# Hybrid mLSTM and RWKV-7 block: who holds the PSUM banks between preparation, join and chain, and how many buffers the modulation loads have

## The chip, the cores and the metric

The kernel runs on one core of a Trainium2 chip. The metric is device time in microseconds (us). A core has five engines with a queue each: TensorE (PE in the rows; PEld is its weight load), VectorE (DVE), ScalarE (ACT), GpSimd (POOL) and SyncE (SP, which issues most transfers). PSUM, the memory that TensorE writes, has eight banks of 512 float32 values per partition.

## The reference, cut to what matters

512 latent tokens and 256 context tokens, width 2048, go through one layer. The part that the change touches is the RWKV-7 head group: 16 heads of 64, scanned forwards and backwards, the context first and then the latent tokens from the context's final state.

```python
sh1, sc1, gt1, sh2, sc2, gt2 = adaln(c, w_mod, b_mod)      # 6 x 2048 values
proj = modulate(rms_norm(x, g1), sh1, sc1) @ w_in
def step(s, xs):                     # per head, per token, in each direction
    r_t, w_t, k_t, v_t, kk_t, a_t = xs
    s = s * w_t - (s @ kk_t) (kk_t * a_t)^T + v_t k_t^T
    return s, s @ r_t
y = group_norm(y_f + y_b) * gn_w + gn_b, plus a bonus, times a gate
x = x + gt1 * (concat(hm, y) @ w_out)     # hm: the mLSTM heads
x = x + gt2 * conv_ffn(modulate(rms_norm(x, g2), sh2, sc2))
return rms_norm(x, g_final)
```

## The kernel before, in words

Instructions are written once in Python. A planner orders them on each engine: it gives each instruction a priority by its place in the program, simulates, and lets a later one run when an earlier one is not ready. Tiles of one tag share a fixed number of buffers, and PSUM banks are such tags: `acc` (2 banks) for the big matrix products, `pre` (4 banks) for everything that prepares the scan, `R` (2 banks) for the scan itself.

The scan goes in chunks of 64 tokens, two heads (a "pair") at a time, eight pairs. A **preparation** (`pair_shared`, `prep`, `bonus`) makes the operands of a pair's chunks in `pre` banks and writes them to a DRAM tensor `S_d`. Its first matmul in a `pre` bank is that of line 669, on the square made at line 667. A **solve** (first half of `tsolve`) inverts 32x32 triangles by 60 small VectorE instructions (lines 798, 799). A **join** (second half of `tsolve`) makes 64x64 inverses of them by 256 small matmuls for two pairs (lines 816, 821), in `R` banks. Solve and join share the one buffer `t_X`. A **chain** (`chain`, `chain_step`) goes through the chunks of two pairs, both directions, one step after the other: 116 matmul instructions of line 859 in two `R` banks, two ScalarE copies (lines 870, 878) and the state's update (line 890) in a step. Its operands come by `chain_load`, two chunks at a time (512 KB for the latent tokens), in six buffers of `r_GK`. **Finishing** a pair (`finalize_pair`, driven by `fin_step`) reads the chain's output back, normalises it, transposes it in a `pre` bank (line 977) and evacuates it (line 978); `chain` calls for the next half of a finish (`mid()`) before its third step and at its end.

The jobs stand in this order in the program (X01 are the latent tokens of pairs 0 and 1; each job ends with what is named last):

| call | before |
|---|---|
| `ctx_job(p)` | chain of the job before last; preparations of p and p+1; solve and join of the job before |
| `x_job(0)`, `(1)` | chain of an earlier context job; preparations 0 and 1; `x_job(0)` ends with solve and join of the last context job |
| `x_job(2)` | solve and join X01; preparation 2 |
| `x_job(3)` | chain X01; preparation 3 |
| `x_job(4)` | solve and join X23; preparation 4 |
| `x_job(5)` | chain X23, with the first finishes (pair 0, half of pair 1); preparation 5 |
| `x_job(6)` | solve and join X45; preparation 6 |
| `x_job(7)` | chain X45, with finishes; preparation 7 |
| after them | solve and join X67; chain X67, with finishes |

Between them stand the projections (`x_pair`, `x_head`, lines 370 to 372 and 403 to 405), which need no scan and fill TensorE, and `ada_late`: a late piece of the modulation, read from `w_mod` in eight 512 KB loads (line 228) through the one buffer `am`, each used by two VectorE instructions (line 232). Five such pieces stand behind the chain X67. Then come the mLSTM heads (lines 605 to 640), the output projection in two halves (line 1268; the first half needs heads 0 and 1 and pairs 0 to 3 only), and the ConvFFN.

Of the kernel before, what the change touches and what calls it, by code (L numbers as in the profile page):

```python
# [9 lines left out]
F32R = mybir.dt.float32r  # L10
# [5 lines left out]
P = 128  # L16
# [24 lines left out]
T_MISC, T_LW, T_LA, T_R, T_KR, T_Q, T_K, T_O, T_LG = 0, 1, 2, 3, 11, 19, 23, 27, 35  # L41
# [55 lines left out]
def body(tc, A, dbg=None):  # L97
# [46 lines left out]
    rk = Pool("rk")  # L144
# [102 lines left out]
        return sm("ev", [P, 512], EVB)  # L247

    def am():
        return sm("am", [P, 2, 512], 1)  # L250

    def rsqrt_big(dst, src, scale, eps_ap, n):
        t = ev()
# [523 lines left out]
    def tsolve(pairs):  # L777

        nc_ = 2 * pairs[0][0].nch
        n = 4 * nc_ * len(pairs)  # L780
        x = rp("t_X", [P, 32, 32], 1)[0:n]

        def blocks():
            q = 0
            for us in pairs:
                for r in range(0, P, 32):
                    o = us[0].kc + r % 64
                    yield x[q:q + nc_], us[0].S_d[r:r + 32, :, o:o + 32].rearrange("s c t -> c s t")
                    q += nc_

        for t, g in blocks():
            sp.dma_start(t, g)
        T1 = rp("t_T", [P, 256], 1)[0:n]
        dve.memset(x.rearrange("p s t -> p (s t)")[:, 0:1024:33], 1.0)
        for t in range(30, 0, -1):
            m = 31 - t
            w = T1[:, 0:t * m].rearrange("p (s t) -> p s t", t=m)
            dve.tensor_tensor(w, x[:, 0:t, t:t + 1].to_broadcast([n, t, m]), x[:, t:t + 1, t + 1:32].to_broadcast([n, t, m]), ALU.mult)
            dve.tensor_tensor(x[:, 0:t, t + 1:32], x[:, 0:t, t + 1:32], w, ALU.add)
        for t, g in blocks():  # L800
            sp.dma_start(g, t)

        XT = rp("t_X", [P, 2, 16, 32], 1)
        for k, us in enumerate(pairs):
            kc = us[0].kc
            T_d = us[0].S_d[:, :, kc:kc + 64]
            T = rp("t_Y", [P, 16, 64], 1)[:, 0:nc_]
            sp.dma_start(T, T_d)
            W = XT[:, k, 0:nc_]
            dve.transpose(W, T[:, :, 0:32])  # L810
            ws = [PS("R", [P, 16, 32])[:, 0:nc_] for _ in range(2)]
            a_, b_ = ([slice(64 * h + o, 64 * h + o + 32) for h in range(2)] for o in (0, 32))
# [12 lines left out]

    def chain_load(u, tt):

        cu = u.c0 + 2 * tt
        o = rk("r_GK", [P, 2, 512], 6)[:, :, 0:3 * u.kc + 128]
        sp.dma_start(o, u.S_d[:, cu:cu + 2, :])  # L830
        return o

    def chain_v(p, seg, nch):
# [70 lines left out]
    def chain(pairs, mid):  # L904

        x = pairs[0][0].seg == "x"
        nch = pairs[0][0].nch
        Vs, ys = [], []
        for us in pairs:
            Vs.append(chain_v(us[0].p, us[0].seg, nch))  # L910
            ys.append(rk("r_yt", [P, 8, 64], 2) if x else None)
            for u in us:
                if not x:
                    Mst[(u.p, u.d)] = rk("r_M", [P, 64], 16)
                    pool.memset(Mst[(u.p, u.d)], 0.0)
                u.M = Mst[(u.p, u.d)]
        n = nch // 2
        for i in range(n):
            if x and i == 1:
                mid()  # L920
            ops = [[chain_load(u, i if u.d == 0 else n - 1 - i) for u in us] for us in pairs]
            for c in range(2 * i, 2 * i + 2):
                units = []
                for k, (us, os_, V, y) in enumerate(zip(pairs, ops, Vs, ys)):
                    us[0].y = y
                    for j, (u, o) in enumerate(zip(us, os_)):
                        cu = nch - 1 - c if j else c
                        units.append((u, o[:, cu % 2], cu, V, 2 * k + (j if 2 * c < nch - 1 else 1 - j)))
                chain_step(units, c < nch // 2, x and c == nch - 1)
        if x:  # L930
            for us, y in zip(pairs, ys):
                y_d = us[0].y_d = DT("yr_d", [4, P, 128], 8)
                for h in range(2):
                    sp.dma_start(y_d[:, :, 64 * h:64 * h + 64].rearrange("a (b t) v -> t (a b) v", t=64), y[LOHI[1 - h]])
            mid()

    def bonus(p, uf, ub, s):
        kd = uf.kd
# [11 lines left out]
    def finalize_pair(p, uf, ub, bo):  # L950
# [21 lines left out]
        gs = sq.rearrange("p a b -> p (a b)")  # L972
        sp.dma_start(gs, g_d[p])
        yield
        pt = PS("pre", [P, 512])
        for tt in range(4):
            pe.transpose(pt[:, 128 * tt:128 * tt + 128], y[:, tt, :], ident)
        dve.scalar_tensor_tensor(gs, pt, V("gnb", p), gs, ALU.add, ALU.mult)
# [31 lines left out]
    ctx_plan = [("r_GK", ("cm", T_LW, T_LA))]  # L1010
    for p in range(0, NPAIR, 2):
        ctx_plan += [("r_GK", ("tm", p // 2)), ("r_GK", ("cm", T_KR + p, T_KR + p + 1))]
    ctx_plan += [("r_GK", ("cm", T_MISC)), ("r_GK", ("cm", T_K, T_K + 1)), ("r_GK", ("cm", T_K + 2, T_K + 3))]
    ctx_plan += [(("r_y", "am")[h // 2], ("tm", 4 + h)) for h in range(MH)]

    def ctx_part(H, k0, k1, part):
        for n, (tag, (kind, *ts)) in enumerate(ctx_plan):
            if k0 == 0:
                if tag == "r_y":
                    d = rk("r_y", [P, 512], 2)  # L1020
                else:
                    if n % 2 == 0:
                        pair = am() if tag == "am" else rk("r_GK", [P, 2, 512], 6)
                    d = pair[:, n % 2]
                part.append(d)
            d = part[n][:, 0:512 if kind == "tm" else NC_ * len(ts)]
            pt = PS("acc", [P, 512])[:, 0:d.shape[-1]]
            part_of(kind, ts, H, k0, k1, pt)
            if k0 == 0:
                act.copy(d, pt)  # L1030
            else:
                dve.tensor_tensor(d, pt, d, ALU.add)
# [56 lines left out]
    for q, (k0, k1) in enumerate(KPARTS):  # L1089
        ks = slice(k0, k1)  # L1090
        n = (k1 - k0) * P
# [22 lines left out]
    Hx = HT(NX)  # L1114
    modulated(xload2, rx, gsc[:, :, 0], mod[:, 0:16], Hx, range(8))

    solve_q, chain_q = [], []

    fin_q = []

# [15 lines left out]
        while fin_q or fin[0] is not None:  # L1136
            fin_step()

    def do_chain(n=1):
        if len(chain_q) >= n:  # L1140
            job = [t for _ in range(n) for t in chain_q.pop(0)]
            chain([us for _, us, _ in job], fin_step)
            fin_q.extend(t for t in job if t[2] is not None)

    def do_solve(n=1):
        if len(solve_q) >= n:
            jobs = [solve_q.pop(0) for _ in range(n)]
            tsolve([us for job in jobs for _, us, _ in job])
            chain_q.extend(jobs)

    def ctx_job(p):
        do_chain()
        job = []
        for pp in range(p, p + 2):
            s = pair_shared(pp, "c")
            job.append((pp, prep(pp, s, "c", DT("Sc_d", [P, 8, 320], 8)), None))
        do_solve()
        solve_q.append(job)

    def x_job(p):  # L1160
        if p < 2:
            do_chain()
        elif p % 2 == 0:
            do_solve(2)
        else:
            do_chain(2)
        s = pair_shared(p, "x")
        S_d = DT("Sx_d", [P, 16, 512], 8)
        us = prep(p, s, "x", S_d, 0) + prep(p, s, "x", S_d, 1)
        job = [(p, us, bonus(p, us[0], us[1], s))]  # L1170
        if p == 0:
            do_solve()
        solve_q.append(job)


    for i, _ in enumerate(ctx_finish(Hc, part)):
# [8 lines left out]
    def x_first():  # L1185
        for i, (pt, f) in enumerate(zip(proj2([A["wcm"][T_LW], A["wcm"][T_LA]], Hx), (AF.Tanh, None))):
            keep(pt, NX, l_d[i], f)
        pm = proj_cm(T_MISC, Hx)
        lh, ll = sm("am", [P, 2, 512], 1, F32R), [sm("adacc", [P, 512], 2, F32R) for _ in range(2)]

        def gate(pt, j):
            t = ev()
# [35 lines left out]
    for p in range(NPAIR):  # L1228
# [12 lines left out]
        for h in range(MH):  # L1241
            if HEAD_AT[h] == p and p < 7:
                x_head(h)
    do_solve(2)
    for h in range(MH):
        if h == CHAIN_H:
            do_chain(2)
        if HEAD_AT[h] == 7:
            x_head(h)
        for _ in range(LATE_H[h]):  # L1250
            ada_late(next(chunks))
        for i in range(NEARLY):
            if EARLY_AT[i] == h:
                run([mlstm_head(i, True)])
# [30 lines left out]
    for k in KORD[:8]:  # L1285
        mix(k)
    run([mlstm_head(h, EARLY_AT[h] == 4 and h < NEARLY) for h in range(MH) if EARLY_AT[h] == 4 or h >= NEARLY] + [out_first()])
    assert not chain_q and not solve_q
    ahead_[0] = AHEAD
    Hm.more(2)  # L1290
    for k in KORD[8:]:
# [215 lines left out]
```

## Time and profile before

| | us |
|---|---|
| median of 3 runs (lowest to highest) | 3405.07 (3402.93 to 3407.92) |
| profiled execution, its own time | 3401.15 |
| its span, first to last instruction | 3399.3 |
| TensorE busy | 3083.4 (91%) |
| VectorE busy | 2170.8 (64%) |
| ScalarE busy | 1181.5 (35%) |

The profile is of one execution. Busy time counts instructions at work, not waits; the clock that was granted to TensorE is given as a share of full speed, its mean over the execution 0.933.

### The profile page before, as it was taken

The page shows a single profiled execution, that of the slowest core. Times are in us where ns is not written, and L with a number is a line of the kernel's source. Part 1 is how long each engine was busy: PE and PEld are TensorE (multiplying, and loading weights), DVE is VectorE, ACT ScalarE, POOL GpSimd, SP SyncE. Part 2 cuts the span into 40 slices and gives each one's busy share as a digit, 9 for nine tenths or more (in the row PEclk, how much of TensorE's full clock was granted, in tenths as well). Part 3 has the DMA queues.
Part 4 walks back from the last instruction along what each step waited for, and adds up shares of the span by engine and source line. Part 5 has one row for each costly group of instructions (what it writes and reads, how often), then busy time and mean ns, then how long its engine had stood idle before and what let it go on. Part 6 is the DMA issues. An engine that isn't in the chain of part 4 may idle for free.

```text
span 3399.3 us, 54225 instructions
## 1 busy us (share of the span) xinstructions
PE 3083.4 (91%) x21030; PEld 2509.1 (74%) x21030; DVE 2170.8 (64%) x4178; ACT 1181.5 (35%) x2235; POOL 45.7 (1%) x113
## 2 busy tenths in 40 slices
PE   8998889999999886576498899999999999999998
PEld 5687777777788774555376688888888888888887
DVE  2577886898764796655554678455555555655657
ACT  4355654344323433133222433222222222322323
POOL 0000000010000000000000000000000000000000
PEclk9999889999999896567798999999999999999999
DMA  8877556677764766667644255222232232223222
GB/s 286 303 238 221 161 161 183 184 227 214 236 197 152 229 215 192 191 193 235 226 141 156 81 190 197 92 97 96 97 96 97 94 99 93 99 93 99 93 99 100
DMA packets 394385, 548.51 MB, mean 161 GB/s; under 512 B 151664, under 2 KB 272776, under 8 KB 393872
## 3 DMA queue, kind: packets, MB, share of 16 engines
q1 hardware_dynamic: 384480, 531.67, 49.2%
q10 hardware_dynamic: 9648, 13.37, 1.1%
q8 instruction: 166, 2.72, 0.3%
q14 instruction: 91, 0.75, 0.1%
HBM read 457.49 MB, written 87.47 MB: 160 GB/s over the span
## 4 chain that ended last, share of the span: by engine, by line
PE 57%; DVE 10%; DMA 9%; issue 2%; ACT 2%; SPq 1%; DVEq 0%; ACTq 0%
PE acc L372 10%; PE acc L370 10%; PE acc L371 10%; PE acc L1382 5%; PE acc L1384 4%; PE acc L1383 4%; DMA am<-in_wmod 3%; PE acc L1268 1%; PE acc L1269 1%; PE acc L1270 1%; DVE adacc L232 1%; DVE r_Gp L750 1%; PE R L859 1%; PE pre L621 1%; DVE r_M L890 1%
## 5 line engine op out<-in xcount | busy, mean ns | idle before, releaser
L299 ACT CAST whi<-wraw 128x512 fp32r<-128x512 f32 (+1 forms) x948 | 569.5, 604 | 1350.4 <-PE acc L371 719.6
L300 DVE TENSOR_TENSOR wlo<-wraw,whi 128x512 fp32r<-128x512 f32 (+1 forms) x948 | 627.9, 666 | 463.9 <-ACT whi L299 446.8
L372 PE MATMUL acc<-H,wlo 128*128 128x512 f32 x1920 | 760.0, 396 | 5.3 <-DVE wlo L300 5.3
L370 PE MATMUL acc<-H,whi 128*128 128x512 f32 x1920 | 758.5, 395 | 1.5 <-ACT upad L1323 0.5
L371 PE MATMUL acc<-H,whi 128*128 128x512 f32 x1920 | 756.9, 394 | 0.0
L372 PEld LDWEIGHTS acc<-H,wlo 128*128 128x128 f32 x1920 | 364.0, 190 | 85.1 <-DVE wlo L300 7.1
L370 PEld LDWEIGHTS acc<-H,whi 128*128 128x128 f32 x1920 | 364.3, 190 | 80.8 <-issue 2.5
L371 PEld LDWEIGHTS acc<-H,whi 128*128 128x128 f32 x1920 | 363.9, 190 | 77.3 <-issue 1.4
L1386 DVE SCALAR_TENSOR_TENSOR x<-acc,mod,x 128x512 f32<-128x512 f32 (+1 forms) x192 | 135.6, 706 | 221.8 <-PE acc L1384 221.7
L1330 DVE SCALAR_TENSOR_TENSOR f_cv<-upad,fvec,f_cv 128x512 f32<-128x512 f32 x352 | 263.8, 749 | 7.2
L1382 PE MATMUL acc<-fh,whi 128*128 128x512 f32 x640 | 253.2, 396 | 0.0
L1383 PE MATMUL acc<-fl,whi 128*128 128x512 f32 x640 | 253.1, 396 | 0.0
L1384 PE MATMUL acc<-fh,wlo 128*128 128x512 f32 x640 | 253.1, 396 | 0.0
L232 DVE SCALAR_TENSOR_TENSOR adacc<-am,csil,adacc 128x512 f32<-128x512 f32 x240 | 179.4, 747 | 92.2 <-DMA am<-in_wmod 90.5
L404 PE MATMUL acc<-whi,H 128*128 128x256 f32 x512 | 151.8, 297 | 0.0
L405 PE MATMUL acc<-wlo,H 128*128 128x256 f32 x512 | 148.9, 293 | 3.1 <-DVE wlo L300 3.1
L403 PE MATMUL acc<-whi,H 128*128 128x256 f32 x512 | 150.5, 294 | 0.5 <-DVE ev L434 0.5
L1384 PEld LDWEIGHTS acc<-fh,wlo 128*128 128x128 f32 x640 | 120.2, 188 | 29.1
L1382 PEld LDWEIGHTS acc<-fh,whi 128*128 128x128 f32 x640 | 120.2, 188 | 29.0
L1383 PEld LDWEIGHTS acc<-fl,whi 128*128 128x128 f32 x640 | 120.2, 188 | 29.0
L750 DVE TENSOR_TENSOR r_Gp<-pre,c_gmask 64x512 f32<-64x512 f32 (+1 forms) x192 | 115.2, 600 | 34.8 <-DMA Sx_d<-r_Gp 21.3
L1268 PE MATMUL acc<-H,whi 128*128 128x512 f32 x256 | 104.3, 410 | 20.9 <-ACT H L299 16.0
(348 smaller groups left out, 4639.8 us busy)
## 6 DMA issues: line engine op xcount, KB each, us to landing
am<-in_wmod SPq DMA_DIRECT2D x128, 512.0 KB
wraw<-in_wup SPq DMA_DIRECT2D x88, 512.0 KB
wraw<-in_wgate SPq DMA_DIRECT2D x88, 512.0 KB
wraw<-in_wdn SPq DMA_DIRECT2D x88, 512.0 KB
wraw<-in_wcm SPq DMA_DIRECT2D x72, 512.0 KB
r_GK<-Sx_d SPq DMA_DIRECT2D x64, 512.0 KB
wraw<-in_wtm SPq DMA_DIRECT2D x56, 512.0 KB
Sx_d<-r_Gp SPq DMA_DIRECT2D x32, 512.0 KB
```

What stands on the lines that cost most here:

```text
L232: dve.scalar_tensor_tensor(acc, wm[:, k % 2], csil[:, k:k + 1], acc, ALU.mult, ALU.add)
L299: act.copy(hi, t)
L300: dve.tensor_tensor(lo, t, hi.bitcast(F32), ALU.subtract)
L370: pe.matmul(pt[:, :n], hi(k8), H.h(k), start=k == 0, stop=False)
L371: pe.matmul(pt[:, :n], hi(k8), H.l(k), start=False, stop=False)
L372: pe.matmul(pt[:, :n], lo(k8), H.h(k), start=False, stop=k == KT - 1)
L403: pe.matmul(o, H.h(k)[:, xs], hi(k4), start=first, stop=False, skip_group_check=True)
L404: pe.matmul(o, H.l(k)[:, xs], hi(k4), start=False, stop=False, skip_group_check=True)
L1330: dve.scalar_tensor_tensor(cv, u[:, a:a + GH, b:b + GW], fvec[:, f, tap:tap + 1], cv, ALU.mult, ALU.add)
L1382: pe.matmul(pt, hi(m)[:, k, :], th[:, cs], start=k == 0, stop=False)
L1383: pe.matmul(pt, hi(m)[:, k, :], tl[:, cs], start=False, stop=False)
L1384: pe.matmul(pt, lo(m)[:, k, :], th[:, cs], start=False, stop=k == GF - 1)
```

## The change

Four edits. Joins become a function of their own, `tjoin`, in `pre` banks. The transposes of finished pairs move from a `pre` bank to an `R` bank, and the second call of `mid()` in a chain from its end to its seventh step. Chain operands are loaded one chunk at a time in ten `r_GK` buffers of half the size. The buffer `am` moves to another pool and becomes two. The order of the jobs changes with it: every `ctx_job` and every odd `x_job` ends with a solve, and the job after it prepares, joins and runs the chain.

| call | after |
|---|---|
| `ctx_job(p)` | preparations of p and p+1; join and chain of the job before; solve of this job |
| `x_job(0)` | preparation 0; join and chain of the last context job |
| `x_job(1)` | preparation 1; solve X01 |
| `x_job(2)` | preparation 2; join and chain X01 |
| `x_job(3)`, `(4)` | preparation 3, solve X23; preparation 4, join and chain X23 |
| `x_job(5)`, `(6)` | preparation 5, solve X45; preparation 6, join and chain X45 |
| `x_job(7)` and after | preparation 7, solve X67; join X67; chain X67 |

```diff
     def am():
-        return sm("am", [P, 2, 512], 1)
+        return rk("am", [P, 2, 512], 2)
...
         for t, g in blocks():
             sp.dma_start(g, t)
 
+    def tjoin(pairs):
+
+        nc_ = 2 * pairs[0][0].nch
         XT = rp("t_X", [P, 2, 16, 32], 1)
...
-            ws = [PS("R", [P, 16, 32])[:, 0:nc_] for _ in range(2)]
+            ws = [PS("pre", [P, 16, 32])[:, 0:nc_] for _ in range(2)]
...
-    def chain_load(u, tt):
-        cu = u.c0 + 2 * tt
-        o = rk("r_GK", [P, 2, 512], 6)[:, :, 0:3 * u.kc + 128]
-        sp.dma_start(o, u.S_d[:, cu:cu + 2, :])
+    def chain_load(u, cu):
+        o = rk("r_GK", [P, 512], 10)[:, 0:3 * u.kc + 128]
+        sp.dma_start(o, u.S_d[:, u.c0 + cu, :])
         return o
...
-        for i in range(n):
-            if x and i == 1:
+        for c in range(nch):
+            if x and c in (2, 6):
                 mid()
...
-            mid()
...
-        pt = PS("pre", [P, 512])
+        pt = PS("R", [P, 512])
         for tt in range(4):
             pe.transpose(pt[:, 128 * tt:128 * tt + 128], y[:, tt, :], ident)
...
     def ctx_job(p):
-        do_chain()
-        job = []
         for pp in range(p, p + 2):
             s = pair_shared(pp, "c")
-            job.append((pp, prep(pp, s, "c", DT("Sc_d", [P, 8, 320], 8)), None))
+            made.append((pp, prep(pp, s, "c", DT("Sc_d", [P, 8, 320], 8)), None))
+        do_join()
+        do_chain()
         do_solve()
-        solve_q.append(job)
 
     def x_job(p):
-        if p < 2:
-            do_chain()
-        elif p % 2 == 0:
-            do_solve(2)
-        else:
-            do_chain(2)
         s = pair_shared(p, "x")
         S_d = DT("Sx_d", [P, 16, 512], 8)
         us = prep(p, s, "x", S_d, 0) + prep(p, s, "x", S_d, 1)
-        job = [(p, us, bonus(p, us[0], us[1], s))]
-        if p == 0:
+        made.append((p, us, bonus(p, us[0], us[1], s)))
+        do_join()
+        do_chain()
+        if p % 2:
             do_solve()
-        solve_q.append(job)
...
-    do_solve(2)
+    do_join()
     for h in range(MH):
         if h == CHAIN_H:
-            do_chain(2)
+            do_chain()
```

Two partial sums of the context's projection move from `r_GK` to `r_yt`, which is free then, because ten half-size buffers hold fewer of them.

## Rows read from the trace of the kernel before

**Rows 1.** Busy time by stretch: from:to, length, engines busy, granted clock, DMA, GB/s.
```profile
340.00:905.00 565.00, 509.06 (x4368) 415.44 (x4367) 470.32 (x1042) 263.02 (x534) 32.85 (x51) 0.94 0.63 191
905.00:1113.00 208.00, 203.39 (x2370) 175.79 (x2371) 111.94 (x264) 65.55 (x123) 0.00 (x0) 0.97 0.61 192
1113.00:1323.00 210.00, 171.99 (x2088) 141.22 (x2087) 158.90 (x345) 77.47 (x155) 4.88 (x9) 0.87 0.71 218
1323.00:1483.00 160.00, 98.04 (x1399) 78.70 (x1399) 107.22 (x272) 44.11 (x93) 0.94 (x5) 0.55 0.59 176
1483.00:1657.00 174.00, 125.92 (x1327) 98.49 (x1327) 98.68 (x251) 61.86 (x158) 1.79 (x8) 0.77 0.75 244
1657.00:1946.00 289.00, 226.73 (x937) 176.09 (x935) 153.51 (x273) 88.90 (x163) 0.00 (x0) 0.88 0.41 133
1946.00:3400.00 1454.00, 1436.10 (x6468) 1185.42 (x6468) 869.25 (x1333) 414.19 (x687) 0.00 (x0) 1.00 0.33 108
```

**Rows 2.** The same view, the chain's matmuls (line 859) alone: PE, PEld, clock, DMA.
```profile
942.00:1092.00 150.00, 21.47 (x928) 17.77 (x928) 0.98 0.54 175
...
1126.00:1295.00 169.00, 22.87 (x928) 18.84 (x921) 0.90 0.70 221
...
1326.00:1449.00 123.00, 47.61 (x928) 42.07 (x928) 0.54 0.59 177
...
1483.00:1658.00 175.00, 35.62 (x928) 30.79 (x928) 0.78 0.75 244
```

**Rows 3.** The same view, projection matmuls of line 370 alone.
```profile
1113.00:1323.00 210.00, 39.93 (x96) 19.24 (x96) 0.87 0.71 218
1323.00:1946.00 623.00, 0.00 (x0) 0.00 (x0) 0.77 0.55 175
```

**Rows 4.** Timeline of ScalarE and VectorE: start, length, engine, line, operation.
```profile
884.04 0.63 ACT L667 ACTIVATE r_t<-r_kk 128x512 f32<-128x512 f32 x1
...
1237.53 0.63 ACT L667 ACTIVATE r_t<-r_kk 128x512 f32<-128x512 f32 x1
...
993.61 0.71 DVE L810 STREAM_TRANSPOSE t_X<-t_Y 128x512 f32<-128x512 f32 x1 [6.91 <-DMA t_Y<-Sx_d]
```

**Rows 5.** Timeline of TensorE around 1093, 1112 and 1321 us.
```profile
1093.77 1.41 PE L816 MATMUL R<-t_X,t_Y 32*32 32x32 f32 x62
...
1111.57 0.60 PE L977 MATMUL pre<-c_ident,r_y 128*128 128x128 f32 x4
1112.01 1.02 PE L669 MATMUL pre<-r_t,c_bones 128*128 128x512 f32 x2
...
1321.17 1.92 PE L669 MATMUL pre<-r_t,c_bones 128*128 128x512 f32 x2
```

**Rows 6.** Busy time by stretch, line 747 alone: the Gram matmuls of preparation 5.
```profile
1112.00:1176.00 64.00, 6.91 (x64) 6.04 (x64) 0.92 0.71 228
```

**Rows 7.** The chain that ended last, in order of time: start, length, what.
```profile
733.84 3.28 DMA am<-in_wmod
...
992.57 7.66 DMA r_GK<-Sx_d
...
1679.57 2.99 DMA r_y<-g_d
```

**Rows 8.** Busy time by stretch, line 798 (solves) alone: DVE, clock, DMA.
```profile
340.00:400.00 60.00, 9.40 (x29) 0.91 0.50 154
...
814.00:890.00 76.00, 9.64 (x29) 0.96 0.66 216
949.00:984.00 35.00, 9.75 (x30) 1.00 0.61 224
```

**Rows 9.** Line 228, 1460 to 1735 us: durations, first and last start; who waited.
```profile
L228 SPq DMA_DIRECT2D am<-in_wmod x39: 327/333/1451, 1468.2 to 1725.2; - x39
...
  DVE adacc L232: 48.9, 23
```

**Rows 10.** Tile r_GK: what TensorE's idle time before its uses ended with (us, times).
```profile
  DMA r_GK<-Sx_d: 30.2, 25
```

More of the change, by code (lines that the diff above doesn't have):

```diff
@@ L916, in chain @@
                 u.M = Mst[(u.p, u.d)]
-        n = nch // 2
-        for i in range(n):
-            if x and i == 1:
+        for c in range(nch):
+            if x and c in (2, 6):
                 mid()
[L921 to L929, printed above, removed]
+            units = []
+            for k, (us, V, y) in enumerate(zip(pairs, Vs, ys)):
+                us[0].y = y
+                for j, u in enumerate(us):
+                    cu = nch - 1 - c if j else c
+                    units.append((u, chain_load(u, cu), cu, V, 2 * k + (j if 2 * c < nch - 1 else 1 - j)))
+            chain_step(units, c < nch // 2, x and c == nch - 1)
         if x:
@@ L1012, in body @@
         ctx_plan += [("r_GK", ("tm", p // 2)), ("r_GK", ("cm", T_KR + p, T_KR + p + 1))]
-    ctx_plan += [("r_GK", ("cm", T_MISC)), ("r_GK", ("cm", T_K, T_K + 1)), ("r_GK", ("cm", T_K + 2, T_K + 3))]
+    ctx_plan += [("r_GK", ("cm", T_MISC)), ("r_yt", ("cm", T_K, T_K + 1)), ("r_yt", ("cm", T_K + 2, T_K + 3))]
     ctx_plan += [(("r_y", "am")[h // 2], ("tm", 4 + h)) for h in range(MH)]
@@ L1018, in ctx_part @@
             if k0 == 0:
-                if tag == "r_y":
-                    d = rk("r_y", [P, 512], 2)
-                else:
-                    if n % 2 == 0:
-                        pair = am() if tag == "am" else rk("r_GK", [P, 2, 512], 6)
-                    d = pair[:, n % 2]
+                if tag == "am":
+                    if n % 2 == 0:
+                        pair = am()
+                    d = pair[:, n % 2]
+                else:
+                    d = rk(tag, [P, 512], 10 if tag == "r_GK" else 2)
                 part.append(d)
@@ L1115, in body @@
     modulated(xload2, rx, gsc[:, :, 0], mod[:, 0:16], Hx, range(8))
-    solve_q, chain_q = [], []
+    made, solved, joined = [], [], []
     fin_q = []
@@ L1137, in do_finalize, with do_chain, do_join, do_solve @@
             fin_step()
-    def do_chain(n=1):
-        if len(chain_q) >= n:
-            job = [t for _ in range(n) for t in chain_q.pop(0)]
+    def do_chain():
+        if joined:
+            job = joined.pop(0)
             chain([us for _, us, _ in job], fin_step)
             fin_q.extend(t for t in job if t[2] is not None)
[L1145 to L1149, printed above, removed]
+    def do_join():
+        if solved:
+            job = solved.pop(0)
+            tjoin([us for _, us, _ in job])
+            joined.append(job)
+    def do_solve():
+        job = list(made)
+        made.clear()
+        tsolve([us for _, us, _ in job])
+        solved.append(job)
     def ctx_job(p):
-        do_chain()
-        job = []
         for pp in range(p, p + 2):
             s = pair_shared(pp, "c")
-            job.append((pp, prep(pp, s, "c", DT("Sc_d", [P, 8, 320], 8)), None))
+            made.append((pp, prep(pp, s, "c", DT("Sc_d", [P, 8, 320], 8)), None))
+        do_join()
+        do_chain()
         do_solve()
-        solve_q.append(job)
     def x_job(p):
-        if p < 2:
-            do_chain()
-        elif p % 2 == 0:
-            do_solve(2)
-        else:
-            do_chain(2)
         s = pair_shared(p, "x")
@@ L1188, in x_first @@
         pm = proj_cm(T_MISC, Hx)
-        lh, ll = sm("am", [P, 2, 512], 1, F32R), [sm("adacc", [P, 512], 2, F32R) for _ in range(2)]
+        lh, ll = rk("am", [P, 2, 512], 2, F32R), [sm("adacc", [P, 512], 2, F32R) for _ in range(2)]
         def gate(pt, j):
@@ L1287, in body @@
     run([mlstm_head(h, EARLY_AT[h] == 4 and h < NEARLY) for h in range(MH) if EARLY_AT[h] == 4 or h >= NEARLY] + [out_first()])
-    assert not chain_q and not solve_q
+    assert not made and not solved and not joined
     ahead_[0] = AHEAD
```

## The prediction

> **What bounds the kernel now.** I read the busy times by stretch first. TensorE is the busiest engine in each, so time can come only from where it waits or runs slowly: before 1113 us and after 1946 us it is nearly full, from 1113 to 1946 us it is not, and from 1323 to 1657 us it works 224 of 334 us at a granted clock of 0.55 and 0.77 [rows 1]. VectorE isn't full there either (206 of 334 us). So a chain of waits sets that stretch. The next view says why nothing fills it: the projections, which need no scan, are used up by 1323 us [rows 3], while two of the four latent chains come after that: they run at 942 to 1092, 1126 to 1295, 1326 to 1449 and 1483 to 1657 us [rows 2].
>
> Why are they so late? Preparation 5 had its square ready at 884 us, but the first matmul in a `pre` bank on it ran at 1112 us, directly behind the transposes of the first finished pair [rows 4, 5]. For preparation 7 it is 1237 us, and 1321 us. Banks of one tag are given out in program order, as these pairs show: the finish stands earlier in the program, and it needs the output of chain X01, which ended at 1092 us. So 228 us of preparation's lead were thrown away there, and 84 us at the other place. The join of X23 shows the same in the other banks: its first VectorE transpose ran at 993.6 us, its matmuls, in `R` banks, at 1093.8 us, behind the chain's last step [rows 4, 5]. Between the chains 34, 31 and 34 us pass with a join and the loads after it.
>
> **The change part by part.** All sums are against the profiled execution, 3401 us (its span is 3399.3); the median is 4 us above it. The path that I follow ends with the chain X67 at 1657 us, and what comes after it until the ConvFFN's start near 1946 us.
>
> *Gaps between chains.* With joins in `pre` banks and finishes in `R` banks, preparations 3 to 7 no longer wait for a chain's end. A preparation takes about 64 us once it can run [rows 6], two with a join's part about 145 us (an estimate: twice 64 and some 17 for the join), a chain 123 to 175 us [rows 2], so operands should lie ready. The three gaps, 99 us, shrink to one landing of operands each, at most 7.7 us [rows 7]: minus 76. Bounds: minus 99, and 0 if joins are late.
>
> *Start of chain X01.* It waits for five solves and joins through the one buffer `t_X`. The solves span 60 us in the first, 76 in the fifth, and 354 in all five, while one that runs almost alone takes 35 [rows 8]. They now stand ahead of the next preparation in the program, so they get VectorE first: at most minus 179. Against it, preparations now queue behind joins in the `pre` banks, and VectorE is 83% busy from 340 to 905 us [rows 1]: at worst 0. I take a third, minus 60.
>
> *The chains themselves.* The third ran in 123 us with little beside it, the others took 150, 169 and 175 [rows 2]. Earlier, it will have projections and preparations beside it: mean of the others, 165, plus 42 (bounds 0 and 52). The fourth had VectorE stalled by modulation loads, 48.9 us of waits in 1460 to 1735 us [rows 9], part of them in its time: minus 15 (0 to minus 49). Loads by chunk: today TensorE waits 30.2 us for operands [rows 10]; ten chunk buffers hold this step's four, the next step's four and two more, where six double ones hold four in use and only two of the next four: minus 15 (0 to minus 30; the loss is a rival below). The extra issues, 96 loads, sit on SP, which mostly waits. Five finishes fall inside chains and each takes an `R` bank from the next step: four transposes, 0.6 us together [rows 5], an evacuation of 0.7 us like the transpose of this size [rows 4], and as much again for handing over, 2.6 us each: plus 13 (0 to 40). Sum: plus 25.
>
> One rule speaks against the smaller loads. Rows first: a 512 KB load landed in 3.28 us, a 256 KB one in 2.99 us, and a 512 KB one of operands took 7.66 us [rows 7], so half the bytes don't take half the time. The Trainium skill, "DMA: Bandwidth & Descriptors", section "Anatomy of one DMA", says the same: about 2.0 us per transfer whatever its size, plus the bytes at 436 GB/s (measured there for transfers that GpSimd issues). By it 96 more transfers would cost an estimated 192 us if they stood one behind the other; hidden, as I take them to be, nothing.
>
> *After the last chain.* The five late pieces of modulation run from 1468 to 1725 us, 39 loads in 257 us, 6.6 us each [rows 9]: load, two VectorE instructions, next load. Heads 2 and 3 and the output projection's evacuations stand behind them in VectorE's queue. With two buffers the next load runs beside the instructions, and 3.3 us a load is seen [rows 7]. The stretch from 1657 to 1946 us has 62 us of idle TensorE [rows 1], and work of the output projection's first half, which could run beside the last chain. Bounds: 0, and minus 111 (the idle time, and VectorE's 48.9 us of waits for these loads); I take minus 50, near the middle. What lies behind 1946 us doesn't change: TensorE is busy there 1436 of 1454 us. The moved partial sums and the two `am` buffers in other uses cost nothing: they lie in stretches where TensorE has other work; uncovered, a ScalarE copy of 0.6 us each.
>
> Sum: minus 76, 60 and 50, plus 25, makes minus 161: 3401 - 161 = 3240, and with the 4 us to the median **3244 us**, rounded 3245.
>
> **The rivals.**
>
> *VectorE sets the pace.* Preparations now wait for the join ahead of them in the `pre` queue, the join for its solve, the solve for `t_X`. If that loop and VectorE's load eat what the order gives, chain X01 starts at 942 us as now, and only the gaps go; the last part gives 25. Minus 76, plus 25, minus 25: 3325 us. For it: VectorE 83% busy early [rows 1], the solves' 354 us where 175 would do [rows 8]. Against: the idle VectorE from 905 to 1113 us, 96 us [rows 1].
>
> *TensorE is the bound at last.* If everything overlaps as well as from 340 to 905 us, where busy time times clock is 0.85 of the stretch, then the work from 340 to 1946 us (the same product summed over these rows, 1176 us) takes 1384 us instead of 1606: minus 222, 3183 us. For it: 905 to 1113 us reaches 0.95. Against: the last chain and the finishes behind it can't be filled wholly.
>
> *Operands come late (slower).* The place is `chain_load` in SP's queue, where it now stands 32 times instead of 16 in front of each latent unit's row of steps, behind loads that wait for buffers. If a step's loads land after the step before has ended, each of the 32 latent steps pays a landing, 7.66 us at most [rows 7]: 245 us, less the 161, gives 3401 + 84 + 4 = 3489 us. It decides from 161/32 = 5.0 us a step. The rule of the Trainium skill above would be its cause. Against: 25 such waits cost only 30.2 us now [rows 10], and there is a whole step's lead.
>
> *It doesn't do what it says.* The `pre` queue gets a new blocker: a join that waits for a late solve holds all preparations, as the finish did. Then the lead is lost again elsewhere, and the time stays near 3400 us.
>
> **How the numbers follow.** The forecast 0.58 (own range 3180 to 3305), VectorE's pace 0.19, TensorE's bound 0.09, no change 0.05, late operands 0.09. The bounds of the terms reach further than these; they'd have to fall on one side together. The range 3150 to 3365 us holds the forecast, nearly all of the second and most of the third: about 0.8. The first three are faster, 0.86; same 0.05; slower 0.09. A measurement here can tell about 0.2% from no change, 7 us.
>
> **What would show it.** Preparation 5's square and its first `pre` matmul a few us apart, near 900 to 1000 us. Joins whose matmuls follow their transposes at once. Latent chains that follow each other within 10 us or so, the first one starting near 880 us and the last one ending near 1520 us. Projection matmuls beside the third chain, and a granted clock above 0.8 there. Late modulation loads 3.5 to 5 us apart. The ConvFFN's start near 1785 us. I would be wrong if preparations stand still behind a join, if TensorE's waits for `r_GK` grow past 100 us, or if the chains' steps grow by more than 5 us.

## The result and the profile after

The median went from 3404.0 us (four runs; the table ahead of the prediction has three of them) to 3370.82 us (3369.3 to 3373.17), a ratio of 0.9904 [0.9887, 0.9922]: 33 us faster, where 159 were forecast. The profiled execution took 3371.52 us, with a span of 3369.7 and a mean granted clock of 0.938.

Set against the terms of the sum: a chain is counted here from its first to its last ScalarE copy of line 870 (872 after), in both kernels, and the ConvFFN's first instruction is at 1946 us before, 1918 after.

| term | forecast, us | measured, us |
|---|---|---|
| gaps between the latent chains | -76 | -16 (156 to 140) |
| start of chain X01 | -60 | -7 (959 to 952) |
| the four chains themselves | +25 | +10 (539 to 549) |
| after the last chain | -50 | -15 (292 to 277) |
| sum | -161 | -28 (the span: -29.6) |

Every term has the sign that was forecast, and an eighth to two fifths of its size. (The split depends on the measure. From the first matmul to the last, as in [rows 2], the gaps are 101 us before and 63 after, the chains 614 and 656, the start comes 13 us earlier and the last part is 19 shorter; the sum is the same. The reason is that 8 of a chain's 928 matmuls run ahead of the rest, 4 to 14 us before the change and 18 to 21 after it: by the program they belong to the first of the chain's two pairs, whose half of the join comes first. The copies come when both pairs are through.)

The next fence shows the busy times by stretch, with the columns and stretches of [rows 1]; the ConvFFN starts 28 us earlier, so the last two rows are cut at 1918.

```profile
340.00:905.00 565.00, 511.56 (x4349) 430.05 (x4348) 413.42 (x940) 233.64 (x476) 35.72 (x41) 0.93 0.58 174
905.00:1113.00 208.00, 182.79 (x2185) 150.38 (x2185) 143.53 (x312) 77.99 (x156) 8.51 (x10) 0.93 0.66 199
1113.00:1323.00 210.00, 185.33 (x2284) 154.12 (x2283) 168.04 (x364) 89.13 (x171) 6.86 (x10) 0.94 0.77 231
1323.00:1483.00 160.00, 88.52 (x1394) 76.81 (x1393) 100.48 (x258) 40.09 (x87) 0.52 (x4) 0.56 0.62 190
1483.00:1657.00 174.00, 136.44 (x1294) 97.17 (x1293) 127.88 (x317) 65.67 (x163) 0.56 (x6) 0.80 0.82 262
1657.00:1918.00 261.00, 231.18 (x978) 185.46 (x977) 137.44 (x243) 92.04 (x169) 1.23 (x2) 0.93 0.44 145
1918.00:3370.00 1452.00, 1435.74 (x6468) 1185.24 (x6468) 868.78 (x1333) 413.92 (x687) 0.00 (x0) 1.00 0.32 108
```

TensorE lost 21 us of work between 905 and 1113 us and found 13 in the stretch behind it; from 1323 to 1483 us it is emptier than before (89 us for 98), at the same low clock. The only clear gain is from 1483 us on.

The four chains by the copies alone, the same view as [rows 2] (ScalarE's busy time, clock, DMA, GB/s), first before, then after:

```profile
959.00:1085.00 126.00, 5.78 (x16) 0.97 0.49 159
1135.00:1287.00 152.00, 5.58 (x16) 0.90 0.68 213
1336.00:1446.00 110.00, 5.50 (x16) 0.53 0.56 168
1503.00:1654.00 151.00, 5.36 (x15) 0.76 0.74 241
```

```profile
952.00:1099.00 147.00, 5.87 (x16) 0.90 0.66 207
1136.00:1281.00 145.00, 5.85 (x16) 0.92 0.74 236
1330.00:1445.00 115.00, 5.84 (x16) 0.56 0.66 215
1499.00:1641.00 142.00, 5.80 (x16) 0.79 0.81 262
```

From the first chain's start to the fourth's it is 544 us before and 547 after: the chains follow each other no faster.

What holds preparations 5 and 7 now? First ScalarE's timeline with their squares, as in [rows 4], then TensorE's, as in [rows 5].

```profile
1054.30 0.63 ACT L667 ACTIVATE r_t<-r_kk 128x512 f32<-128x512 f32 x1
...
1250.30 0.63 ACT L667 ACTIVATE r_t<-r_kk 128x512 f32<-128x512 f32 x1 [0.84 <-DVE r_BK L733]
```

```profile
1115.00 1.20 PE L819 MATMUL pre<-t_X,t_Y 32*32 32x32 f32 x64
...
1117.43 1.10 PE L669 MATMUL pre<-r_t,c_bones 128*128 128x512 f32 x2
...
1308.52 1.20 PE L819 MATMUL pre<-t_X,t_Y 32*32 32x32 f32 x64
...
1310.95 1.10 PE L669 MATMUL pre<-r_t,c_bones 128*128 128x512 f32 x2
```

The squares are ready at 1054 and 1250 us, and the first `pre` matmuls on them run at 1117 and 1311, each directly behind matmuls of line 819, which are those for the second of a join's two pairs. The finish has left the `pre` queue and the join has taken its place. The cost is 63 and 61 us of lead, less than the 228 and 84 us before, but it now comes around with every second preparation: 1117 to 1311 us are 194 us for two preparations. That round can be read off in four pieces. Preparation 5 runs from 1117 to 1183 us, where preparation 6 has its first matmul. The solve that needs preparation 5 runs from 1194 to 1273 us. Then t_Y has to be read back from DRAM (VectorE's first transpose of the join is at 1284.5), and the matmuls of line 819 for the join's second pair end near 1310, with the preparation's behind them at 1311. The solves, line 798 alone, as in [rows 8] (the fifth, and those beside preparations 4 and 6):

```profile
834.00:891.00 57.00, 9.64 (x29) 0.95 0.58 188
1002.00:1079.00 77.00, 9.75 (x30) 0.91 0.64 216
1194.00:1273.00 79.00, 9.77 (x30) 0.91 0.62 205
```

In their early part the solves became faster, as forecast: the first five span 256 us for 354. Beside an even preparation a solve takes 77 to 79 us, of which line 798 is 10. VectorE's timeline shows an instance of what stretches it:

```profile
1195.44 0.25 DVE L798 TENSOR_TENSOR t_T<-t_X 128x84 f32<-128x84 f32 x1
1195.61 0.75 DVE L232 SCALAR_TENSOR_TENSOR adacc<-am,csil,adacc 128x512 f32<-128x512 f32 x1
1196.27 0.24 DVE L799 TENSOR_TENSOR t_X<-t_X,t_T 128x84 f32<-128x84 f32 x1
```

Each of the 60 small instructions needs the one before, and where a long one gets in between, 0.25 us become 0.8.

Last the late modulation loads [rows 9] and the waits for operands [rows 10]:

```profile
L228 SPq DMA_DIRECT2D am<-in_wmod x38: 327/333/745, 1480.3 to 1670.1; - x38
...
  DVE adacc L232: 21.2, 18
```

```profile
  DMA r_GK<-Sx_d: 20.7, 14
```

The loads come 5.0 us apart (190 us for 38) instead of 6.6, and VectorE's wait fell from 48.9 to 21.2 us. TensorE waits 20.7 us for operands instead of 30.2.

### The profile page after: what moved, and what is told of

It is laid out like the page before. It is cut to its first block, busy times and chain, and to the rows that moved or that the text cites. A ratio compares the mean times of both kernels' runs of the same rounds, so it can differ in the third digit from the quotient of the medians.

```text
span 3369.7 us, 54393 instructions
## 1 busy us (share of the span) xinstructions
PE 3081.6 (91%) x21030; PEld 2518.3 (75%) x21030; DVE 2165.6 (64%) x4178; ACT 1182.0 (35%) x2237; POOL 58.4 (2%) x113
## 4 chain that ended last, share of the span: by engine, by line
PE 48%; DMA 6%; DVE 5%; ACT 2%; issue 1%; SPq 1%; POOL 0%; DVEq 0%; ACTq 0%
PE acc L370 9%; PE acc L372 9%; PE acc L371 9%; PE acc L1380 5%; PE acc L1381 5%; PE acc L1382 5%; DMA am<-in_wmod 2%; PE acc L1266 1%; PE acc L1268 1%; PE acc L1267 1%; DVE adacc L232 1%; DMA x_d<-ev 1%; DMA wraw<-in_wdn 0%; DVE r_M L892 0%; PE R L861 0%
```

## The experiments

Two theories. A: the join is the new blocker in the `pre` queue, and the order of the jobs lets it wait for its solve; the other edits give what they should. B: TensorE, VectorE or the loads by chunk set the pace, and who holds which bank hardly matters. All medians stand against the kernel before on the same chip (3402 to 3406 us); each interval is some 5 to 8 us to either side.

**Joins back in `R`**, all else as after.

```diff
-            ws = [PS("pre", [P, 16, 32])[:, 0:nc_] for _ in range(2)]
+            ws = [PS("R", [P, 16, 32])[:, 0:nc_] for _ in range(2)]
```

> The changed kernel with the joins in R banks again. Theory A (the queue for the pre banks): in the changed kernel each odd preparation waits in the pre queue behind a join, the join behind its solve, the solve behind the odd preparation before it, some 190 us for two pairs. Without joins in that queue preparation 1 makes its first matmul near 690 us instead of 750, preparation 5 near 960 to 1000 instead of 1117, and chain X01 starts 40 to 90 us earlier than 950; joins wait for the chain before them again, so gaps between chains stay near 35 us. 3310 to 3345 us. Theory B (the buffer t_X and VectorE's load set the pace, wherever the preparations stand): preparations move, chains start within 15 us of where they do now, 3365 to 3400 us.

3330.55 us, 0.9781 [0.9767, 0.9796]: 40 us faster than after. TensorE's timeline:

```profile
901.86 1.12 PE L669 MATMUL pre<-r_t,c_bones 128*128 128x512 f32 x2
...
1057.76 1.20 PE L669 MATMUL pre<-r_t,c_bones 128*128 128x512 f32 x1
...
1134.80 1.85 PE L819 MATMUL R<-t_X,t_Y 32*32 32x32 f32 x62
```

Preparations 5 and 7 run at 902 and 1058 us, 216 and 253 us earlier, and from preparation 3 on each takes 68 to 79 us. The join of X23 now waits for chain X01 in the `R` banks (chain's end 1127, join 1135). The chains start at 969, 1196, 1366 and 1480 us by their copies, the first two later than after, the last two closer behind each other, and the ConvFFN starts at 1879 us. By the copies the last chain ends only 9 us earlier (1631 us for 1640); the other 30 are won behind it (248 us to the ConvFFN for 278). So the edit of the join's banks, taken alone, costs 40 us in this order. That part of theory A holds; its earlier start of the chains doesn't.

**Finishes back in `pre`**, all else as after.

```diff
-        pt = PS("R", [P, 512])
+        pt = PS("pre", [P, 512])
```

> The changed kernel with the transposes of finished pairs in pre banks again. Theory A: preparation 5 stands behind the second half of the first finish, which now comes in the seventh step of chain X23 near 1240 us, so its first matmul moves from 1117 to about 1260 us, the last chain ends 60 to 130 us later: 3420 to 3490 us. Theory B: 3365 to 3385 us, preparations stay where they are.

3425.4 us, 1.0062 [1.0045, 1.0078]: 55 us slower than after. TensorE's timeline:

```profile
1121.48 0.60 PE L975 MATMUL pre<-c_ident,r_y 128*128 128x128 f32 x4
...
1122.73 1.10 PE L669 MATMUL pre<-r_t,c_bones 128*128 128x512 f32 x2
...
1716.49 1.11 PE L975 MATMUL pre<-c_ident,r_y 128*128 128x128 f32 x4 [11.09 <-DVE r_y L969]
1717.40 1.91 PE L605 MATMUL pre<-r_kr,r_KR 128*128 128x512 f32 x2
```

Preparation 5 stands right behind a finish, but at 1123 us, only 5 us later than behind the join (1117). Preparation 7 stands behind one too and comes 27 us later (1338), yet the last chain ends as before (1642 us for 1640). The price is paid after the last chain: heads 2 and 3 (line 605) start behind the last finish at 1717 us, where after has them from 1596 us on, beside the chain. The size came as expected, at another place.

**One `am` buffer again**, all else as after.

```diff
-        return rk("am", [P, 2, 512], 2)
+        return sm("am", [P, 2, 512], 1)
...
-        lh, ll = rk("am", [P, 2, 512], 2, F32R), [sm("adacc", [P, 512], 2, F32R) for _ in range(2)]
+        lh, ll = sm("am", [P, 2, 512], 1, F32R), [sm("adacc", [P, 512], 2, F32R) for _ in range(2)]
```

> The changed kernel with one am buffer, in its old pool. If the second buffer gave the shorter tail (19 us) and the shorter chains (34 us): 3395 to 3425 us. If the loads are hidden now or were never on the path: 3365 to 3380 us. Late modulation loads go back to about 6.6 us each in either case.

3424.43 us, 1.0055 [1.004, 1.007]: 54 us slower than after. Line 228 from 1460 us on:

```profile
L228 SPq DMA_DIRECT2D am<-in_wmod x41: 327/333/1126, 1466.7 to 1768.8; - x41
...
  DVE adacc L232: 54.4, 27
```

The loads end at 1769 us instead of 1670, 7.4 us apart, VectorE waits 54.4 us for them, and the ConvFFN starts at 1965 us, 47 later. Of these, 31 us lie ahead of the last chain's end (1671 us for 1640) and only 16 behind it. The second buffer is worth more than the 33 us that the whole change brings.

**The kernel before with its finishes in `R`**, nothing else: the one line of the second experiment, the other way round.

> The kernel before with the transposes of finished pairs in R banks, that edit alone. Theory A: preparation 5 is freed from 1112 us to 905 to 960 us, preparation 7 to about 1100; joins still wait for the chain before, gaps stay near 34 us, but chains run earlier from X45 on: 3330 to 3385 us. Theory B: the third and fourth chain move by under 15 us, 3390 to 3410 us.

3359.85 us, 0.9857 [0.9835, 0.9879]: 45 us faster than before, and 11 faster than the whole change. TensorE's timeline:

```profile
908.12 1.78 PE L669 MATMUL pre<-r_t,c_bones 128*128 128x512 f32 x2 [0.37 <-DVE r_Gp L750]
...
1065.58 1.12 PE L669 MATMUL pre<-r_t,c_bones 128*128 128x512 f32 x2
```

Preparation 5 comes at 908 us for 1112, preparation 7 at 1066 for 1321. The reading of [rows 4, 5], that the finish held them, is shown. Yet the last chain's copies end only 19 us earlier (1635 us for 1654). The rest behind it is 22 us shorter (270 for 292), and there the same line frees heads 2 and 3, which start at 1576 us instead of 1697. So the 45 us are not the preparations' alone.

**Join and chain behind the odd preparation.** A job's join then stands a preparation later in the `pre` queue, when its solve should be done.

```diff
         made.append((p, us, bonus(p, us[0], us[1], s)))
-        do_join()
-        do_chain()
         if p % 2:
+            do_join()
+            do_chain()
             do_solve()
```

> The changed kernel with join and chain of the latent pairs placed behind the odd preparation only, so that a preparation more stands between a solve and the join that waits for it; joins stay in pre banks. Theory A (preparations wait behind joins in the pre queue): preparation 5 makes its first matmul near 960 us, preparation 7 near 1090, chain X01 starts at 890 to 920 us, the gaps between chains fall below 12 us, the last chain ends at 1530 to 1570 us, the time is 3270 to 3310 us. Theory B (t_X, the solves and VectorE set the pace whatever the queue): chain X01 starts at 940 us or later, the last chain ends at 1620 us or later, 3320 us or more.

3308.72 us, 0.9727 [0.9705, 0.9749]: 62 us faster than after, with the same banks, loads and buffers. Preparations 5 and 7 run at 1011 and 1194 us, 106 and 117 us earlier. The chains by their copies:

```profile
962.00:1103.00 141.00, 5.35 (x15) 0.90 0.71 228
1138.00:1284.00 146.00, 5.83 (x16) 0.89 0.78 247
1328.00:1423.00 95.00, 5.52 (x16) 0.58 0.62 187
1445.00:1590.00 145.00, 5.61 (x16) 0.76 0.80 265
```

The first three start as after. The last one follows 22 us behind X45 instead of 54 and starts 54 us earlier: preparation 7 is through so much sooner that the last solve ends at 1376 us for 1445. The place of the join sets that, as A says. But of what A expected only the time came: chain X01 starts where B had it, and the gaps (35, 44 and 22 us) are far from A's 12. The join now stands ahead of the even preparations instead: the square of preparation 6 is ready at 1063 us and waits until 1113.

**Join and chain behind preparations 1, 2, 5 and 7**: the join of X01 early, the others late.

```diff
-        do_join()
-        do_chain()
+        if p in (1, 2, 5, 7):
+            do_join()
+            do_chain()
```

> The same, but join and chain X01 stay behind preparation 2 as in the changed kernel; the joins of the last context job, X23 and X45 stand behind preparations 1, 5 and 7. Theory A: preparation 1 no longer waits for the last context join, solve X01 runs near 750 to 810 us, chain X01 starts at 850 to 890 us, the last chain ends at 1520 to 1560 us, 3255 to 3300 us. Theory B: chain X01 at 940 us or later, 3320 us or more.

3327.44 us, 0.9776 [0.9759, 0.9793]: 19 us slower than the order above, and short of what was expected. Chain X01 starts at 921 us, 41 earlier, but the join of X23 comes at 1116 instead of 1084 us and the last chain ends at 1607 instead of 1590. An earlier first chain was paid back at the second.

**Solves without their elimination** (56 of 60 instructions of each left out), all else as after.

```diff
-        for t in range(30, 0, -1):
+        for t in (2, 1):
```

> The changed kernel without 56 of the 60 VectorE instructions of each solve (two steps of the elimination are left, so the inverses are wrong). Theory A: preparations wait for joins only because joins wait for solves; with the solve's 45 to 78 us gone a join is ready when the even preparation ends, preparations 3, 5 and 7 follow each other at 130 to 150 us per two instead of 187 to 195, chain X01 starts near 800 us, and the time is 3230 to 3300 us. Theory B (VectorE's own load and the length of a preparation set the pace): two preparations still take 165 us or more, 3310 to 3350 us.

3270.37 us, 0.9601 [0.9583, 0.9619]. Chain X01 starts at 833 us by its copies, 119 earlier, and the last ends at 1455. TensorE's timeline at preparations 5 and 7:

```profile
961.44 1.19 PE L819 MATMUL pre<-t_X,t_Y 32*32 32x32 f32 x62
...
963.48 1.10 PE L669 MATMUL pre<-r_t,c_bones 128*128 128x512 f32 x2
...
1145.23 1.20 PE L669 MATMUL pre<-r_t,c_bones 128*128 128x512 f32 x1
```

Preparation 5 still stands behind a join, and two preparations still take 182 us here, 154 in the round before (810 to 963). Both theories missed a part: the solves are worth 100 us, as A says, but the round isn't theirs alone. And even with solves nearly free the time isn't below the 3245 us of the forecast: the last chain ends 65 us earlier than forecast (1455 for 1520), but 358 us follow until the ConvFFN where the forecast had 265, and TensorE is busy in 313 of them.

**Loads of two chunks again** (five buffers of two chunks, which is the same memory as ten of one), all else as after.

```diff
-        o = rk("r_GK", [P, 512], 10)[:, 0:3 * u.kc + 128]
-        sp.dma_start(o, u.S_d[:, u.c0 + cu, :])
-        return o
+        if not hasattr(u, "ops"):
+            u.ops = {}
+        tt = cu // 2
+        if tt not in u.ops:
+            o = rk("r_GK", [P, 2, 512], 5)[:, :, 0:3 * u.kc + 128]
+            c0 = u.c0 + 2 * tt
+            sp.dma_start(o, u.S_d[:, c0:c0 + 2, :])
+            u.ops[tt] = o
+        return u.ops[tt][:, cu % 2]
...
```

> The changed kernel with chain operands loaded two chunks at a time again, in five buffers of double size (the same memory). If loads by chunk gained the 15 us that the prediction put down for them, TensorE's waits for r_GK rise by 15 to 40 us and the time to 3380 to 3410 us; if the transfers' fixed cost ate it, 3345 to 3365 us; if chains wait for joins anyway, 3366 to 3376 us.

3351.66 us, 0.9842 [0.9825, 0.9859]: 19 us faster than after. The tile of the operands, first after, then here (shortest, median and longest issue in ns), and what TensorE waited for here:

```profile
L832 SPq DMA_DIRECT2D r_GK<-Sx_d x128: 319/396/2586, 918.5 to 1616.4; - x128
```

```profile
L837 SPq DMA_DIRECT2D r_GK<-Sx_d x64: 319/388/2363, 894.4 to 1607.9; - x64
...
  DMA r_GK<-Sx_d: 22.5, 22
```

The issue of a load takes SP about as long for half the bytes, so by the medians SP spends 78 us on 192 issues after (128 of 0.396, 64 of 0.422) and 40 us on 96 here (the other 32 at 0.460). TensorE's waits for operands are no shorter than after (22.5 us for 20.7): the gain isn't there. Nor is it at the last chain's end, 1640 us in both; the rest behind it is 26 us shorter (252 us for 278).

**Both: join behind the odd preparation, loads of two chunks.**

> The changed kernel with two edits: join and chain behind the odd preparation (alone: 3308.7 us) and chain operands two chunks at a time (alone: 3351.7 us, 19 us under the changed kernel). Theory A (two separate costs, the wait in the pre queue and SP's issue time): they add up, 3280 to 3300 us. Theory B (the smaller loads only cost something because SP delays the joins that the preparations wait for): without that wait nothing is left to gain, 3303 to 3320 us.

3294.2 us, 0.9667 [0.9648, 0.9687]: the fastest version with the reference's whole computation, 77 us faster than after and 110 faster than before. The loads bring 14.5 us here, as theory A had it. The last chain ends 45 us later than with loads by chunk (1634 us for 1590), and the rest behind it is 53 us shorter (211 for 264): when the last chain ends doesn't say by itself when the ConvFFN starts.

**Joins in `R`, loads of two chunks**: the first experiment's line on top of the loads of two chunks.

> The changed kernel with joins in R banks (alone 3330.6 us) and two-chunk loads (alone 3351.7 us). Theory A: the smaller loads cost SP's time wherever joins stand, 3305 to 3318 us. Theory B: 3325 to 3335 us, since preparations no longer wait for joins.

3333.61 us, 0.9787 [0.9767, 0.9806], the same as with loads by chunk (3330.55). With joins in `R` the size of the loads makes no difference. This is theory B's case, the experiment above is A's: neither account of the loads holds in both.

**The old order of jobs** with finishes in `R`, two `am` buffers in the new pool, five `r_GK` buffers of two chunks, and joins in `R`: the kernel before with two of the four edits, and the smaller `r_GK` that makes room for them.

> The kernel before with two of the four edits: finishes in R banks, two am buffers; the old order of jobs, joins in R banks, two-chunk loads (five double buffers, for the memory). Beside e12 it differs in the order of jobs alone. Theory A (what costs time is a wait in the pre queue; the order of solves and preparations gains nothing by itself): 3320 to 3345 us, as e12. Theory B (solves ahead of the next preparation start the chains earlier, as the prediction had it with 60 us): 3370 us or more.

3321.2 us, 0.9753 [0.973, 0.9776]: 50 us faster than the whole change. Against the experiment above, it differs by the order of the jobs and by where a chain calls for its second half finish: these cost some 12 us where joins are in `R`, at the edge of the noise (0.9753 [0.973, 0.9776] against 0.9787 [0.9767, 0.9806]).

So from before to after the edits add up like this: finishes in `R`, 3404 to 3360; two `am` buffers (and the smaller `r_GK`), to 3321; the new order of jobs, to 3334 (some 12 us worse); loads by chunk, to 3331; joins in `pre`, to 3371.

One view puts all versions on one scale: TensorE's busy time from 340 us to the ConvFFN's start, by the busy times by stretch.

| kernel | stretch, us | TensorE busy | idle |
|---|---|---|---|
| before | 1606 | 1335 | 271 |
| finishes in `R` alone | 1565 | 1324 | 241 |
| after | 1577 | 1335 | 242 |
| finishes back in `pre` | 1624 | 1332 | 292 |
| one `am` buffer | 1625 | 1354 | 271 |
| two-chunk loads | 1551 | 1324 | 227 |
| joins in `R`, two-chunk loads | 1541 | 1320 | 221 |
| joins back in `R` | 1538 | 1328 | 210 |
| old order, two edits | 1533 | 1324 | 209 |
| join behind 1, 2, 5 and 7 | 1525 | 1327 | 198 |
| join behind the odd preparation | 1513 | 1332 | 181 |
| join behind the odd one, two-chunk loads | 1505 | 1331 | 174 |
| no elimination | 1472 | 1305 | 167 |

The busy time stays within 20 us of 1335 (but in the last row); what differs is the idle time. The forecast asked for a stretch of 1445 us, some 110 of them idle, and no version comes near that.

## Why the prediction was wrong

**Who holds the banks before** was right. The finish held preparations 5 and 7: with its one line alone they come 204 and 255 us earlier. That line is worth 45 us on its own, heads 2 and 3 included; the 55 us the other way round are the heads'. Joins no longer wait for a chain's banks either: after the change their matmuls follow the transposes at once, as forecast (1284.5 and 1285.3 us for the join of X45).

**The step that failed** is in *Gaps between chains*: "preparations 3 to 7 no longer wait for a chain's end" is true, but "two with a join's part about 145 us (an estimate: twice 64 and some 17 for the join) ..., so operands should lie ready" left the solve out. It was taken to be hidden beside the even preparation. But the odd preparation queues behind the join in the `pre` banks, the join needs the solve, and the solve needs the odd preparation before: 66 us of preparation, 11 to the solve, 79 of solve, 38 for reading back and the join make the 194 us measured. The last rival, "a join that waits for a late solve holds all preparations", had this mechanism, with a chance of 0.05 and a time near 3400 us; the first named the same loop. The prediction's own sign of being wrong, "if preparations stand still behind a join", is what came. With the join out of that queue (3331) or a preparation later in it (3309), the time falls. All four measured terms lie inside the bounds that the prediction gave them, but gaps, start and last part fell short together. It held that to be unlikely ("they'd have to fall on one side together"); gaps and start have one cause in common, joins in the `pre` queue.

How much of it is the solve? From preparation 3 to 5 and from 5 to 7 it takes, by their first matmuls, 188 and 194 us after, 154 and 182 without the elimination, 152 and 183 with the join a preparation later, and 138 and 156 with joins in `R`. So of the 50 and 38 us that joins in `pre` add, about 34 and 12 are the wait for the solve. The rest comes with the join itself: from its first matmul to that of the preparation behind it 23 to 33 us pass (906 to 929, 1089 to 1117 and 1285 to 1311 us after; 936 to 963 and 1112 to 1145 without the elimination), where the forecast had 17. The estimate of 64 us for a preparation was also too small for one that nothing holds: in the first experiment each takes 68 to 79 us.

**Start of chain X01** was forecast at 60 us earlier and came 7 earlier. The solves did shrink, by 98 us for five. That was given back one step on: preparation 1 has its first `pre` matmul at 750 us, where before it ran at 628 and in the first experiment, with joins in `R`, at 618. It stands behind the last context job's join (matmuls until 735 us) and behind transposes of the mLSTM gates (line 474, 748 to 750). The solve of X01, which needs it, starts at 834 us, 20 later than before (814). The buffer `t_X` isn't what held it:

```profile
735.57 2.86 SPq L792 DMA_DIRECT2D t_X<-Sx_d  x4
...
825.07 1.97 SPq L792 DMA_DIRECT2D t_X<-Sx_d  x4
```

This is SP's timeline of the loads into `t_X` for that solve: the first half goes out right behind the join, the second, which reads what preparation 1 made, some 90 us later. With joins in `R` the join of the last context job waits for a context chain instead (chain's end 772, join 778, solve 814 in the first experiment), and chain X01 starts at 969. Only without the elimination (833) or with the join of X01 put early (921) is it more than 21 us earlier than after (952).

**The chains themselves** were forecast at +25 and came at +10, for partly other reasons. The third was to grow by 42 us with work beside it and grew by 5: little came beside it, as preparations were late and the projections were used up. The first grew by 21. The fourth is 9 us shorter, the forecast having 15 for the modulation loads.

**After the last chain** was forecast at -50 and came at -15. The second `am` buffer does work there, but of what it is worth only 16 us lie behind the last chain, as the third experiment shows. What the step missed is that heads 2 and 3 stood behind the last finish in the `pre` queue as well, not only behind VectorE. The trace of before shows it, TensorE's timeline:

```profile
1695.60 1.12 PE L977 MATMUL pre<-c_ident,r_y 128*128 128x128 f32 x4 [14.90 <-DVE r_y L971]
1696.51 4.47 PE L605 MATMUL pre<-r_kr,r_KR 128*128 128x512 f32 x5
```

Finishes in `R` free the heads (1576 us in the fourth experiment), and in the new order the second `am` buffer is needed too: they start at 1596 us after, with one buffer at 1674. But the output projection's second half still waits for the last chain's pairs, and that chain ended 9 us earlier by its matmuls, not 137. The sum also took the chain's end and the rest behind it for separate terms. They aren't: without the elimination the last chain ends 185 us earlier than after (1455 for 1640), but more work is left behind it, 358 us with TensorE busy in 313, instead of 278 with 248.

**Loads by chunk** were put at -15 inside the chains. TensorE's waits fell by 9.5 us, but with two-chunk loads in the changed kernel they are 22.5 us, so less than 2 of these come from the smaller loads; and as such the loads cost 19 us with joins in `pre` (14.5 with the later join), and nothing with joins in `R`. The rival *Operands come late* did not occur: the waits fell. The rule that was weighed there, in the Trainium skill, "DMA: Bandwidth & Descriptors", section "Anatomy of one DMA", gave an estimate of 192 us if the transfers stood one behind the other; the runs show 0 to 19, so nearly all of it was hidden. What costs the 19 us stays open. SP's 38 us of extra issues are the candidate, as a join's read-back goes through SP's queue too and preparations wait for a join only where it is in `pre`. But in the profiled executions the 26 us are won behind the last chain, and no run separates SP's time from the rest.

The Trainium skill, "Perfetto Trace Analysis", section "Identifying Performance Opportunities", says that consistent bubbles on the engine that should be full can mean that there isn't enough PSUM for the next tile. This case agrees in part: the bubbles came from PSUM, but the number of banks was the same in all versions, and no run shows what more of them would give. Who stands in which pool, and in what order, was worth 45 us (finishes), 40 (joins' banks) and 62 (joins' place).

## What to carry to other kernels

Before a consumer is moved into another pool, write down the round that it closes there: who stands behind it in that pool, what it waits for, and whether that wait leads back to one of those behind it; the sum over that round, with every wait at its length beside other work, is the pace, not the sum of the pieces that seem to be left. Time each of several edits alone: here two small edits were worth 83 us, and the larger rest lost 50 of it. An idle engine's total over a stretch is a good check on a forecast, too: it tells how much idleness the forecast would have to remove.

## What the runs showed of the hardware

A chain with little beside it was faster at the lower clock than one with much beside it at the higher: in the first experiment the third chain's matmuls took 89 us at a granted clock of 0.50 (the 1.2 GHz level; TensorE was busy 56 of them), the first one's 160 us at 0.92 (busy 138). So what stood beside a chain counted for more here than the clock; what the third chain would take at the full clock no run shows.

SP's issue of a load took 0.40 us in the median for 256 KB (after) and 0.39 us for 512 KB (loads of two chunks), with single ones up to 2.6 us.
